# Attention in a hybrid decoder block on Trainium2: four of the six q and k copies between partition halves as DMAs from ScalarE's queue

## The chip, the cores and the metric

The kernel runs on one core of one Trainium2 chip. The metric is the device time of one execution in microseconds (us); less is better. Of the kernel before there are three timed runs and one profiled execution.

## The reference, cut to what matters

One decoder block over 1024 tokens of width 1024, in float32. Three groups of heads share one input projection: a gated short convolution, a stick-breaking attention (8 heads of 64), and a spatial gating unit. Their outputs are joined and projected, then follow a feed-forward block of width 4096 with a squared ReLU, and a gated layer embedding. The change lies in the attention:

```python
q = rms_norm(q.reshape(bsz, s_len, ATTN_HEADS, HEAD_DIM), q_norm_g[i])
k = rms_norm(k.reshape(bsz, s_len, ATTN_HEADS, HEAD_DIM), k_norm_g[i])
...
z = jnp.einsum('bqhd,bkhd->bhqk', qi, kj) * scale
t_pos = start + jnp.arange(Q_BLOCK)[:, None]
s_pos = jnp.arange(end)[None, :]
causal = s_pos < t_pos
log_beta = jax.nn.log_sigmoid(z)
log_rem = jnp.where(causal, jax.nn.log_sigmoid(-z), 0.0)
suffix = lax.cumsum(log_rem, axis=3, reverse=True) - log_rem
weights = jnp.where(causal, jnp.exp(log_beta + suffix), 0.0)
o = jnp.einsum('bhqk,bkhd->bqhd', weights, vj)
```

The kernel takes suffix products of sigmoid(−z) with a scan instead of sums of logarithms.

## The kernel before, in words

**Precision.** TensorE multiplies numbers of a reduced float32 format (fp32r). A float32 value is split into a high part (a ScalarE copy that rounds, L134 or L137) and a low part (a VectorE subtraction, L135 or L138). A product of two split values is three matmuls, high·high, low·high and high·low (`product`, L161 to L163).

**Head pairs.** The 8 heads are worked on in 4 pairs. `project(pr)` loads the weights of a pair (SP's queue, 8 loads of 128x384, L66) and computes for each of 8 blocks of 128 tokens the columns of q, k and v into a PSUM bank `qkv_ps` (24 matmuls). ScalarE squares (L338), VectorE sums, POOL takes the power −1/2 (`rs`, L169), VectorE scales q and k (`qk`, L346). V is split straight from the bank (ScalarE L137, VectorE L138); only then is the bank free. There are two such banks.

**Turning q and k.** After every second block, `turn_qk` transposes q and k of two blocks on TensorE into a PSUM bank `qk_tr`, so that the partitions hold the 2 × 64 head dimensions: head 0 in partitions 0 to 63 (`lo_p`), head 1 in 64 to 127 (`hi_p`). It writes the high parts of q to `QS[0]`, the low parts to `low_q`, the high parts of k to `KH[0]`, and the low parts of k to `KL` (VectorE, L371), whose other half is zero.

**The operands of z.** z = q·k needs three products per head, over 64 dimensions each, but the array has 128 rows. So two products are stacked in one matmul: for each head a tile `QS` holds q's high part in one half of the partitions and q's low part in the other, and `KH` holds k's high part in both. z is then QS·KH (L409) plus QS·KL (L411), and a mask matmul (L415). To stack them, parts must move from one half of the partitions to the other. That is the place of the change, reached once per head pair and half of the tokens (`t % 4 == 3`), 8 times. The eight places lie near 105, 127, 167, 200, 237, 270, 306 and 345 us. Before, six copies of 64x512 are done there, three on ScalarE (L375 to L377) and three on VectorE (L378 to L380). Four of the six change partitions: L376 and L377, L379 and L380. L375 and L378 stay in the same partitions.

**Attention.** `attend(pr)` goes through 8 steps (2 heads × 4 groups of two blocks). `stick` makes z in a PSUM bank (two banks `z`), two sigmoids on ScalarE (L416, L417), a scan on VectorE (L421) and a product on POOL or VectorE (L424). `gather` transposes the weights (`w_tr`, L446), splits them (L134, L135) and multiplies with V (`av`, L464). ScalarE copies the result to `y_both` (L473), POOL adds its two halves by a DMA (L475), SP stores it (L395).

**Other transfers in that time.** `block_sums` prepares sums of the last weights in DRAM: 16 copies of 1 MB from ScalarE's queue (`w_sums<-in_w_ff`, L300) and 16 adding transfers of 1 MB from POOL's queue (L297), tied to the steps of `attend`. SP's queue loads weights into a ring of 7 `stage` tiles (L66).

**The order of work.** The Python code weaves `attend(pr)` with the fill, `project(pr + 1)` and at last the convolution, by counts of matmuls. A scheduler then reorders the instructions of each engine by a model of time. So what an engine does next is fixed in the program, and each engine works through its own row in order. DMAs are issued by an engine's sequencer in that same order. A DMA of SP's or ScalarE's queue reports its end on one of 8 counters, DMAHW0 to DMAHW7, which the program deals out in turn; a DMA that gets a counter waits until the last transfer on that counter has landed, and the engine that issues it waits with it.

Of the kernel before, what the change touches and what calls it, by code (L numbers as in the profile page):

```python
# [7 lines left out]
F32 = mybir.dt.float32  # L8
# [24 lines left out]
def hybrid_block(ctx: ExitStack, tc: tile.TileContext, a: dict):  # L33
# [5 lines left out]
    nc = tc.nc  # L39
# [42 lines left out]
    def bank(pool, s):  # L82
        return pool.tile([P, HT], F32, tag=pool.name, name=name(s))
# [47 lines left out]
    def split(src, hi, lo, scale=None, low=nc.vector):  # L131

        if scale is None:
            nc.scalar.copy(hi, src)  # L134
            low.tensor_tensor(out=lo, in0=src, in1=hi, op=ALU.subtract)  # L135
        else:
            nc.scalar.activation(hi, src, AF.Copy, scale=scale)  # L137
            nc.vector.scalar_tensor_tensor(out=lo, in0=src, scalar=scale, in1=hi,  # L138
                                           op0=ALU.mult, op1=ALU.subtract)
# [91 lines left out]
    lo_p, hi_p = slice(0, HD), slice(HD, P)  # L231
# [75 lines left out]
    def project(pr):  # L307
# [11 lines left out]
        for t in range(KT):  # L319
# [34 lines left out]
            if t % 2 == 1:  # L354
                later(72, lambda t=t, qk=qk: turn_qk(heads[pr], t, qk))

    def turn_qk(head, t, qk):

        QS, KH, KL, _, low_q = head
        th = t // 4  # L360
        tr = bank(ps_tr, "qk_tr")
        for i in range(2):
            for j in range(2):
                o = j * 256 + i * P
                nc.tensor.transpose(tr[:, o:o + P], qk[:, i, j * P:(j + 1) * P], ident)
        ws = slice((t % 4 - 1) * P, (t % 4 + 1) * P)

        split(tr[:, :256], QS[0][th][:, ws], low_q[th][:, ws], scale=gq)
        nc.scalar.activation(KH[0][th][:, ws], tr[:, 256:], AF.Copy, scale=gk)
        for hh, own in enumerate((lo_p, hi_p)):  # L370
            nc.vector.scalar_tensor_tensor(out=KL[hh][th][own, ws], in0=tr[own, 256:],  # L371
                                           scalar=gk[own], in1=KH[0][th][own, ws],
                                           op0=ALU.mult, op1=ALU.subtract)
        if t % 4 == 3:
            nc.scalar.copy(KH[1][th][hi_p], KH[0][th][hi_p])  # L375
            nc.scalar.copy(KH[1][th][lo_p], KH[0][th][hi_p])  # L376
            nc.scalar.copy(KH[0][th][hi_p], KH[0][th][lo_p])  # L377
            nc.vector.tensor_copy(QS[1][th][hi_p], QS[0][th][hi_p])  # L378
            nc.vector.tensor_copy(QS[1][th][lo_p], low_q[th][hi_p])  # L379
            nc.vector.tensor_copy(QS[0][th][hi_p], low_q[th][lo_p])  # L380
        return 8

    PROJECT = KT * 72 + 32
# [310 lines left out]
    def fetch(src, tag="raw"):  # L694
        t = late_slot(tag, "raw")
        nc.sync.dma_start(t, src)
        return t
# [142 lines left out]
    for h in range(2):  # L840
        for n in (0, 4, 1, 5, 2, 6, 3, 7):
# [11 lines left out]
            if h == 0:  # L853
                i = len(y_parts[1])
                src = fetch(y_dram[i, 1], "sum") if i < 6 else y_a[i - 6][1]
# [262 lines left out]
```

## Time and profile before

| | us |
|---|---|
| Timed runs, median | 1238.73 |
| Timed runs, lowest and highest | 1237.89, 1245.04 |
| Profiled execution, its time | 1241.13 |
| Profiled execution, span | 1239.4 |
| TensorE busy in the span | 1208.5 |
| VectorE busy | 869.2 |
| ScalarE busy | 605.0 |
| POOL busy | 357.4 |

The mean granted TensorE clock of the span is 0.985 of full speed. The attention takes roughly the stretch from 105 to 370 us; what follows (output projection, feed-forward block, embedding) is not touched. In the rows of the profile PE is TensorE's matmuls, PEld its weight loads, DVE VectorE, ACT ScalarE, POOL GpSimd, SP SyncE; a name with q (ACTq) is the engine's sequencer. "out<-in" are the program's tile names, "<-DVE QS L380" behind an idle time is what ended it. A row of DMA issues gives the time of the issue, and under it the time from issue to landing, as minimum, median and maximum.

### The profile page before, as it was taken

How to read it: one execution, taken by the hardware profiler on the slowest of the kernel's cores; microseconds unless marked ns; L12 is line 12 of the kernel's file. 1: busy time of each engine (PE TensorE's matmuls, PEld its weight loads, DVE VectorE, ACT ScalarE, POOL GpSimd, SP SyncE). 2: the span in 40 equal slices, each digit the busy share in tenths (PEclk: the TensorE clock that was granted, in tenths of full speed). 3: DMA queues.
4: the chain of work that ended last, by engine and by line, in shares of the span. 5: the costliest groups of instructions: out<-in, count | busy, mean ns of one | idle time of the engine just before them, and what ended most of it. 6: DMA issues, size and time to landing. Idle time of an engine off the chain costs nothing.

```text
span 1239.4 us, 17510 instructions
## 1 busy us (share of the span) xinstructions
PE 1208.5 (98%) x5868; PEld 1032.3 (83%) x5868; DVE 869.2 (70%) x1268; ACT 605.0 (49%) x1199; POOL 357.4 (29%) x361
## 2 busy tenths in 40 slices
PE   8999899999999999889999999999999999999998
PEld 7899899898988788678888888888888888888887
DVE  7846888878789655767877678687665555796443
ACT  7736766667565365643333433355453444455211
POOL 2324335465322223235535435321000000022110
PEclk9999999999999999989999999999999999999999
DMA  8602349998631398799999999868865664643221
GB/s 293 237 18 96 117 159 262 246 184 148 129 75 35 116 298 225 205 231 264 269 260 241 254 251 244 234 232 283 327 212 195 199 218 161 224 157 96 83 103 51
DMA packets 119754, 236.46 MB, mean 191 GB/s; under 512 B 13392, under 2 KB 20816, under 8 KB 119408
## 3 DMA queue, kind: packets, MB, share of 16 engines
q1 hardware_dynamic: 94848, 168.08, 40.7%
q0 software_dynamic: 24304, 50.49, 20.6%
q10 hardware_dynamic: 512, 16.78, 3.7%
q8 instruction: 46, 0.75, 0.2%
q14 instruction: 44, 0.36, 0.1%
HBM read 176.57 MB, written 78.64 MB: 206 GB/s over the span
## 4 chain that ended last, share of the span: by engine, by line
PE 85%; DVE 6%; issue 3%; DMA 3%; POOL 2%; ACT 2%; SPq 0%; POOLq 0%; DVEq 0%; ACTq 0%
PE d_ps L752 25%; PE f_ps L752 24%; PE qkv_ps L161 3%; PE qkv_ps L162 3%; PE qkv_ps L163 3%; PE g_ps L161 2%; PE g_ps L163 2%; PE g_ps L162 2%; DVE rem L421 2%; PE av L464 2%; PE w_tr L446 2%; PE o_ps L161 1%; PE o_ps L162 1%; PE o_ps L163 1%; PE cv_ps L161 1%
## 5 line engine op out<-in xcount | busy, mean ns | idle before, releaser
L135 DVE TENSOR_TENSOR w_lo<-raw,w_hi 128x512 fp32r<-128x512 f32 x268 | 240.7, 900 | 94.4 <-ACT w_hi L134 93.1
L134 ACT CAST w_hi<-raw 128x512 fp32r<-128x512 f32 x268 | 164.9, 619 | 241.2 <-PE d_ps L752 119.2
L752 PE MATMUL f_ps<-hn_hi,w_hi 128*128 128x512 f32 x448 | 176.5, 394 | 5.0 <-ACT v L905 5.0
L752 PE MATMUL f_ps<-hn_lo,w_hi 128*128 128x512 f32 x448 | 175.8, 392 | 0.0
L752 PE MATMUL f_ps<-hn_hi,w_lo 128*128 128x512 f32 x448 | 175.3, 392 | 0.0
L752 PE MATMUL d_ps<-f_hi,w_hi 128*128 128x512 f32 x448 | 174.3, 389 | 0.0
L752 PE MATMUL d_ps<-f_lo,w_hi 128*128 128x512 f32 x448 | 174.3, 389 | 0.0
L752 PE MATMUL d_ps<-f_hi,w_lo 128*128 128x512 f32 x448 | 174.3, 389 | 0.0
L421 DVE TENSOR_TENSOR_SCAN rem<-rem 128x128 f32<-128x128 f32 (+3 forms) x64 | 91.5, 1434 | 19.5 <-ACT rem L416 18.5
L752 PEld LDWEIGHTS f_ps<-hn_hi,w_hi 128*128 128x128 f32 x448 | 85.0, 190 | 23.4 <-ACT v L905 5.5
L752 PEld LDWEIGHTS f_ps<-hn_hi,w_lo 128*128 128x128 f32 x448 | 85.1, 190 | 18.0
L740 POOL TENSOR_TENSOR S<-S,sq 128x512 f32<-128x512 f32 x14 | 20.5, 1463 | 275.7 <-ACT sq L809 275.7
L752 PEld LDWEIGHTS f_ps<-hn_lo,w_hi 128*128 128x128 f32 x448 | 85.1, 190 | 17.8 <-issue 0.2
L752 PEld LDWEIGHTS d_ps<-f_lo,w_hi 128*128 128x128 f32 x448 | 84.1, 188 | 17.6
L752 PEld LDWEIGHTS d_ps<-f_hi,w_hi 128*128 128x128 f32 x448 | 84.1, 188 | 17.4
L752 PEld LDWEIGHTS d_ps<-f_hi,w_lo 128*128 128x128 f32 x448 | 84.1, 188 | 17.3
L161 PE MATMUL qkv_ps<-whi,xn_hi 128*128 128x384 f32 x256 | 92.5, 361 | 1.9 <-DVE V L138 1.8
L162 PE MATMUL qkv_ps<-wlo,xn_hi 128*128 128x384 f32 x256 | 89.8, 351 | 0.0
L163 PE MATMUL qkv_ps<-whi,xn_lo 128*128 128x384 f32 x256 | 89.3, 349 | 0.0
L135 DVE TENSOR_TENSOR f_lo<-raw,f_hi 128x512 fp32r<-128x512 f32 x112 | 78.6, 731 | 4.2 <-ACT f_hi L134 3.9
L134 ACT CAST f_hi<-raw 128x512 fp32r<-128x512 f32 x112 | 67.1, 620 | 17.0 <-DMA raw<-f_dram 13.8
L424 POOL TENSOR_TENSOR wt<-wt,rem 128x127 f32<-128x127 f32 (+4 forms) x40 | 45.9, 1156 | 82.7 <-DVE rem L421 40.6
(220 smaller groups left out, 2650.3 us busy)
## 6 DMA issues: line engine op xcount, KB each, us to landing
raw<-in_w_ff SPq DMA_DIRECT2D x160, 256.0 KB, 4.1
raw<-f_dram SPq DMA_DIRECT2D x112, 256.0 KB, 4.6
raw<-w_sums SPq DMA_DIRECT2D x64, 256.0 KB, 3.7
f_dram<-f SPq DMA_DIRECT2D x48, 256.0 KB, 4.6
f_dram<-t SPq DMA_DIRECT2D x48, 256.0 KB, 4.1
w_sums<-in_w_ff POOLq DMA_DIRECT2D x8, 1024.0 KB, 11.4
w_sums<-w_sums POOLq DMA_DIRECT2D x8, 1024.0 KB, 12.3
raw<-in_w_ff POOLq DMA_DIRECT2D x32, 256.0 KB, 5.1
```

Source lines behind the costliest of these rows:

```text
L134: nc.scalar.copy(hi, src)
L135: low.tensor_tensor(out=lo, in0=src, in1=hi, op=ALU.subtract)
L161: nc.tensor.matmul(ps, lh, rh, start=first and i == 0, stop=False)
L162: nc.tensor.matmul(ps, lh, rl, start=False, stop=False)
L163: nc.tensor.matmul(ps, ll, rh, start=False, stop=last and i == len(terms) - 1)
L421: nc.vector.tensor_tensor_scan(out=back, data0=back, data1=back, initial=1.0, op0=ALU.mult, op1=ALU.bypass)
L424: done = (nc.vector if on_vector else nc.gpsimd).tensor_tensor(out=wt[:, :W - 1], in0=wt[:, :W - 1], in1=rem[:, 1:W], op=ALU.mult)
L446: nc.tensor.transpose(tr[:, n:n + P], wts[i][:, kb * P:(kb + 1) * P], ident)
L464: nc.tensor.matmul(av[:, first * P:], lhs, part[:, o:o + m], start=kb == 0 and part is hi, stop=kb == 2 * g + 1 and part is lo)
L740: return eng.tensor_tensor(out=out, in0=x, in1=y, op=ALU.add)
L752: nc.tensor.matmul(bank, l, r, start=first and k == 0 and i == 0, stop=k == len(b) - 1 and i == 2, skip_group_check=True)
```

## The change

Of the six copies the two that stay in their partitions (L375 and, now on ScalarE, `QS[1][hi_p]`) are ScalarE copies. The four that change partitions become DMAs of 64x512 float32 (128 KB), all issued by ScalarE's queue. One of them, `KH[1][lo_p]`, now reads the tile that the first ScalarE copy has just written. VectorE keeps none of the six. Nothing else in the source is changed.

```diff
         if t % 4 == 3:
             nc.scalar.copy(KH[1][th][hi_p], KH[0][th][hi_p])
-            nc.scalar.copy(KH[1][th][lo_p], KH[0][th][hi_p])
-            nc.scalar.copy(KH[0][th][hi_p], KH[0][th][lo_p])
-            nc.vector.tensor_copy(QS[1][th][hi_p], QS[0][th][hi_p])
-            nc.vector.tensor_copy(QS[1][th][lo_p], low_q[th][hi_p])
-            nc.vector.tensor_copy(QS[0][th][hi_p], low_q[th][lo_p])
+            nc.scalar.copy(QS[1][th][hi_p], QS[0][th][hi_p])
+
+            for to, src in ((KH[1][th][lo_p], KH[1][th][hi_p]), (KH[0][th][hi_p], KH[0][th][lo_p]),
+                            (QS[1][th][lo_p], low_q[th][hi_p]), (QS[0][th][hi_p], low_q[th][lo_p])):
+                nc.scalar.dma_start(to.bitcast(F32), src.bitcast(F32))
```

The scheduler moves other work in answer. The rows below are the engines' orders at two of the eight places; a number behind a tile's name tells its copies apart, and the waits are those that the program sets. The copies of the change are rows L375 to L377 before, and L375, L376 and L380 after.

ScalarE at the fourth place (second head pair, second half of the tokens), before:

```order
L369 ACTIVATE KH_1801<-qk_tr_2279,c_gk 128x256 [waits DVE_49]
L375 COPY KH_1805<-KH_1801 64x512 [waits Activation_49]
L376 COPY KH_1805<-KH_1801 64x512
L377 COPY KH_1801<-KH_1801 64x512 [waits DVE_49,Activation_49]
L137 ACTIVATE V_2372<-qkv_ps_2265,r_566 128x2x64 [waits DVE_49]
L134 CAST wT_hi_2437<-w_tr_2432 128x512 [waits PE_49]
```

and after:

```order
L369 ACTIVATE KH_1801<-qk_tr_2279,c_gk 128x256 [waits DVE_49]
L375 COPY KH_1805<-KH_1801 64x512 [waits Activation_49]
L376 COPY QS_1804<-QS_1802 64x512
L380 DMA QS_1804<-q_lo_1803 64x512 [waits DMAHW1_49]
L380 DMA KH_1805<-KH_1805 64x512 [waits DMAHW2_49,Activation_49]
L380 DMA KH_1801<-KH_1801 64x512 [waits DMAHW3_49,DVE_49]
L380 DMA QS_1802<-q_lo_1803 64x512 [waits DMAHW5_49,Activation_49]
L137 ACTIVATE V_2372<-qkv_ps_2265,r_566 128x2x64
L473 COPY y_both_2386<-av_87 128x256 [waits PE_49]
```

Four DMAs, each with a wait for a counter, now stand between the copies and V. The transfers that used counters 1, 2, 3 and 5 last before them are, in SP's order after, the loads of stage_3109, stage_3115, stage_3121 and stage_4001. TensorE at the same place, before:

```order
L446 MATMUL w_tr_2447<-ident,wt_2328 128x128 [waits PE_49]
L446 MATMUL w_tr_2447<-ident,wt_2338 128x128 x2
L409 MATMUL z_2390<-KH_1801,QS_1802 128x128 [waits DVE_49,Activation_49]
L411 MATMUL z_2390<-KL_1797,QS_1802 128x128
L415 MATMUL z_2390<-below,ident 128x128
L409 MATMUL z_2396<-KH_1406,QS_1802 128x512
L411 MATMUL z_2396<-KL_1402,QS_1802 128x512
L161 MATMUL qkv_ps_2469<-whi_2210,xn_hi_197 128x384 [waits DVE_49]
```

and after (the 24 matmuls of qkv_ps_2469 and some others lie in the piece left out):

```order
L446 MATMUL w_tr_2447<-ident,wt_2328 128x128 [waits PE_49]
L446 MATMUL w_tr_2447<-ident,wt_2338 128x128 x2
L161 MATMUL qkv_ps_2469<-whi_2210,xn_hi_197 128x384 [waits DVE_49]
...
L464 MATMUL av_87<-wT_hi_2451,V_1700 128x128
L464 MATMUL av_87<-wT_lo_2452,V_1700 128x128
L409 MATMUL z_2390<-KH_1801,QS_1802 128x128 [waits DMAHW5_49,DMAHW3_49]
L411 MATMUL z_2390<-KL_1797,QS_1802 128x128
```

The first z of the place has moved back by 32 rows, from row 1024 of TensorE to row 1056, behind the next block's qkv_ps, whose bank is the one that V_2372 empties. TensorE at the sixth place (third pair, second half), before:

```order
L161 MATMUL qkv_ps_3346<-whi_3087,xn_hi_197 128x384 [waits DVE_49]
L162 MATMUL qkv_ps_3346<-wlo_3088,xn_hi_197 128x384
L163 MATMUL qkv_ps_3346<-whi_3087,xn_lo_198 128x384
L409 MATMUL z_3287<-KH_2674,QS_2675 128x128 [waits Activation_49]
L411 MATMUL z_3287<-KL_2670,QS_2675 128x128
```

and after:

```order
L161 MATMUL qkv_ps_3346<-whi_3087,xn_hi_197 128x384 [waits DVE_49]
L162 MATMUL qkv_ps_3346<-wlo_3088,xn_hi_197 128x384
L163 MATMUL qkv_ps_3346<-whi_3087,xn_lo_198 128x384
...
L464 MATMUL av_87<-wT_lo_3358,V_2578 128x128
L409 MATMUL z_3287<-KH_2674,QS_2675 128x128 [waits DMAHW5_49,DMAHW4_49]
L411 MATMUL z_3287<-KL_2670,QS_2675 128x128
```

Here z has moved back by 28 rows, from 1442 to 1470, and waits for two of the four transfers.

## The prediction

> **What bounds the kernel now.** I read the page's busy shares first, then busy time by stretches, because the change works only in the first third of the span: the copies in question run from about 105 to 347 us.
>
> ```profile
> PE 1208.5 (98%) x5868; PEld 1032.3 (83%) x5868; DVE 869.2 (70%) x1268; ACT 605.0 (49%) x1199; POOL 357.4 (29%) x361
> 118.00:345.00 227.00, 215.42 (x1328) 203.00 (x1326) 186.63 (x285) 149.35 (x378) 104.81 (x103) 0.95 0.74 183
> 198.00:218.00 20.00, 19.02 (x125) 18.04 (x123) 15.49 (x23) 14.64 (x38) 8.46 (x9) 1.00 0.80 241
> 220.00:230.00 10.00, 7.99 (x40) 7.51 (x40) 9.56 (x12) 4.18 (x10) 3.55 (x4) 0.83 1.13 207
> ```
>
> A window's row gives its length, then busy PE, PEld, DVE, ACT and POOL with their counts, the granted TensorE clock, the DMA share and GB/s. Over the span TensorE is full. In the attention stretch (second row) it stands 227.00 − 215.42 = 11.6 us in all, and the clock there is 0.95. All that a faster VectorE can give back lies in those 11.6 us and that clock. VectorE is 82% busy there, ScalarE 66%, so VectorE is the tighter of the two helpers, and in single windows (last row: 9.56 of 10) it is the bound. Next come the waits of TensorE between 100 and 350 us (total, times, longest):
>
> ```profile
> PE w_tr L446 <- DVE KL L371: 3.7, 3, 1.7
> PE qkv_ps L161 <- DVE V L138: 1.8, 1, 1.8
> PE z L409 <- DVE QS L380: 1.0, 1, 1.0
> ```
>
> Only the last names a removed copy directly. The others may stand behind one, which the chain of waits tells (start, us, engine, line):
>
> ```profile
> 199.42 0.42 DVE QS L379
> 200.33 0.43 DVE QS L380
> 200.90 0.30 PE z L409
> ...
> 269.76 0.35 DVE QS L378
> 270.13 0.43 DVE QS L379
> 270.59 0.42 DVE QS L380
> ...
> 271.45 0.65 PE qkv_ps L161
> ...
> 306.80 0.91 DVE QS L378
> 307.73 0.42 DVE QS L379
> ```
>
> So VectorE's copies lie on the path at three of the eight places (four head pairs, two halves of the tokens): the fourth, near 200 us, the sixth, near 270, and the seventh, near 307.
>
> **The change, part by part.** *Removed.* Per place three VectorE copies and, net, one of ScalarE's three go:
>
> ```profile
> L376 ACT CAST KH<-KH x8: 617/618/621, 105.3 to 345.7; 64x512 fp32r<-64x512 f32 x8
> L378 DVE CAST QS<-QS x8: 419/420/983, 105.8 to 344.4; 64x512 fp32r<-64x512 f32 x8
> ```
>
> VectorE loses 24 × 0.42 = 10.1 us of work. That is the ceiling of the gain. Most of it is not on the path. What is: at the sixth place 0.35 + 0.43 + 0.42 = 1.2 us, since TensorE's 1.8 us wait for V at 271.45 has the three copies ahead of V on VectorE; at the seventh 0.91 + 0.42 = 1.3 us. The fourth place's 1.0 us is dealt with below. Credit: −2.5 us.
>
> *Added on ScalarE.* Four issues of DMAs of 128 KB per place. The trace of before has no such transfer between partitions from ScalarE's queue. The nearest rows are ScalarE's own issues of 1 MB transfers, and SP's stores of the same 64x512 shape:
>
> ```profile
> L300 ACTq DMA_DIRECT2D w_sums<-in_w_ff x16: 496/548/1101, 117.8 to 241.4; - x16
> DMA to landing us min/median/max: 5.8/7.9/10.7
> ...
> L395 SPq DMA_DIRECT2D y_dram<-y_both x12: 445/451/777, 137.5 to 350.1; - x12
> DMA to landing us min/median/max: 2.2/2.7/8.6
> ```
>
> An issue takes about 0.55 us of ScalarE's order of work, so ScalarE goes from three copies (1.85 us) to two copies and four issues (1.24 + 2.2 = 3.4 us): 1.6 us more a place. ScalarE is busy 14.64 of 20 us around the fourth place; this hides. A landing is bounded by 2.2 from below and 10.7 from above. In a quiet stretch I take 2.7, the same shape's median. Before, z needed 3 × 0.42 us of copies; now it needs a landing, so the program's order has put z later, behind 28 to 32 other matmuls at the fourth and sixth places. These cover a short landing.
>
> The Trainium skill ("DMA: Bandwidth & Descriptors", section "Anatomy of one DMA — SWDGE (gpsimd) path") fits a transfer as 2.0 us plus its bytes over 436 GB/s, which makes 2.3 us of 128 KB, an estimate by that page. The trace agrees where the engines are idle (2.2 us at least) and not in the two jams below; by the page alone both would cost nothing, and the time of the first rival below would hold.
>
> *The fourth place: a wait for a completion counter.* In the changed order ScalarE's four issues wait for counters 1, 2, 3 and 5, and the transfers that hold these are SP's loads of the next weights. When these landed before:
>
> ```profile
> L66 SPq DMA_DIRECT2D stage<-in_w_qkv x2: 328/368/407, 190.2 to 190.6; - x2
> DMA to landing us min/median/max: 7.0/10.7/14.4
> ...
> L66 SPq DMA_DIRECT2D stage<-in_w_qkv x2: 328/368/407, 190.6 to 191.3; - x2
> DMA to landing us min/median/max: 14.4/15.0/15.5
> ...
> L66 SPq DMA_DIRECT2D stage<-in_w_conv x1: 382/382/382, 192.2 to 192.2; - x1
> DMA to landing us min/median/max: 15.5/15.6/15.8
> ...
> L137 ACT ACTIVATE V<-qkv_ps,r x1: 367/367/367, 200.3 to 200.3; 128x128 fp32r<-128x128 f32 x1
> ```
>
> The last of the four holders, the load of in_w_conv, landed at 192.2 + 15.5 = 207.7. ScalarE reaches the issues at about 199.5, so it would stand there for 8 us. Queued right behind is V (last row: 200.3 before), which empties the PSUM bank that the next qkv_ps needs, and the next qkv_ps now stands ahead of z on TensorE. So: 207.7, + 0.5 for the issue, + 0.4 for V on ScalarE, + 0.4 for V's low part on VectorE = 209.0. TensorE's first new work was z at 200.90; it now is qkv_ps at 209.0: **+8.1**, in which before's 1.0 us is already replaced. Then the clock. After the 1.8 us stand at 271.45 it was:
>
> ```profile
> 271.00:274.00 3.00, 2.55 (x8) 2.39 (x9) 2.27 (x6) 2.12 (x7) 1.03 (x1) 0.59 1.13 208
> 274.00:277.00 3.00, 3.00 (x16) 2.97 (x15) 1.73 (x2) 1.34 (x3) 0.45 (x1) 0.84 1.13 207
> ```
>
> That is 3 × 0.41 + 3 × 0.16 = 1.7 us lost: **+1.7**. Some comes back: while TensorE stands, VectorE and POOL catch up, and the next stall that VectorE causes, the 2.0 us of the window 220 to 230 above, can shrink or vanish: between 0 and −2.0; I take **−2.0**, as VectorE has far more slack than that in 8 us. Fourth place: +7.8. The bounds are a load that lands before 199.5 (−1.0, the old stall gone) and none of it given back (+9.8).
>
> *The sixth place: the transfers' own landing.* Here z waits for them in a jam that POOL's adding 1 MB transfers make:
>
> ```profile
> 257.60 2.46 POOL L297 DMA_DIRECT2D w_sums<-w_sums  x2
> ...
> L297 POOL DMA_DIRECT2D w_sums<-w_sums x8: 1069/1263/1817, 224.5 to 380.3; - x8
> DMA to landing us min/median/max: 8.0/12.0/22.1
> ...
> L66 SPq DMA_DIRECT2D stage<-in_w_conv x8: 327/328/382, 250.3 to 258.1; - x8
> DMA to landing us min/median/max: 2.4/2.5/7.4
> ...
> 269.41 0.62 ACT L376 CAST KH<-KH 64x512 fp32r<-64x512 f32 x1
> 272.53 0.31 PE L409 MATMUL z<-KH,QS 128*128 128x128 f32 x1
> ```
>
> POOL's second add of that pair, issued about 258.8, lands about 22.1 later, at 280.9; the windows above show a DMA share of 1.13 through 277. SP's load issued as this begins took 7.4 us, where its fellows took 2.5. ScalarE's second copy ended at 270.0; three issues later, at about 271.5, the fourth goes out. By the 7.4 it lands at 278.9, by the 10.7 at 282.2. z is due at 272.5 − 1.2 (the credit) + 28 × 0.17 (the rows moved ahead of it; the 198 to 218 row has 19.02/125 = 0.15, the 274 to 277 row, at a clock of 0.84, 3.00/16 = 0.19) = 276.1. So TensorE stands between 2.8 and 6.1 us; four transfers at once rather than one load speak for more than 2.8, and I take the middle, **+4.5**. The clock after this stand costs what it costs now after the 1.8 us one: 0.
>
> *The other places.* At the second, ScalarE waits for counters held by SP's loads again:
>
> ```profile
> L66 SPq DMA_DIRECT2D stage<-in_w_qkv x2: 328/538/747, 119.3 to 119.7; - x2
> DMA to landing us min/median/max: 8.8/8.8/8.8
> ```
>
> These land by 128.5, about 1 us after ScalarE comes; between 0 and 1: **+0.5**. At the first, third, fifth and eighth places z comes late enough after the copies to cover a 2.7 us landing: 0.
>
> *Sum.* +7.8 (fourth) + 4.5 (sixth) + 0.5 (second) − 2.5 (credits) = +10.3 us. The profiled execution took 1241.13 us (span 1239.4); it would be 1251.4. That execution is 2.4 us over the median of the runs shown, 1238.73; on the median I predict **1249.0 us**.
>
> **The rivals.** *Both waits are hidden, and the freed VectorE shows.* If SP's loads of the fourth place land before 199.5, as the first of them did (190.2 + 7.0 = 197.2), and ScalarE's queue is served at the sixth as in a quiet stretch (2.7 us: 274.2, ahead of 276.1), only gains are left: −2.5 and the 1.0 us stall for QS, −3.5: 1235.2 us. For it speaks that the order of loads can shift by microseconds when ScalarE's own 1 MB transfers go out at other moments; against it, that three of the four loads landed between 205 and 208, not by chance but behind POOL's and ScalarE's megabytes.
>
> *ScalarE's transfers stay behind POOL's until the jam ends; slower than I forecast.* At the sixth place z then waits until 280.9 + 2.2 = 283.1, a stand of 7.0 instead of 4.5; with TensorE stopped twice for so long, POOL's adds, whose starts hang on ScalarE's and POOL's own work, run later too, and the stall of 220 to 230 stays (+2.0). Sum +14.8: 1253.5 us, slower than before by 1.2%. It decides as soon as the fourth transfer takes over 11 us. For it: the 22.1 us landing, and the loads that took 15 near 192. Against: the 7.4 of SP's load in the same jam.
>
> *The change moves nothing.* ScalarE gets to the issues later than I think, so that its stand is short, and the freed VectorE time meets other waits (ScalarE's sigmoids): 1238.7 us. The trace speaks against it only through the order of the program, which puts V straight behind the waits.
>
> **How the numbers follow.** My forecast 0.43, hidden waits 0.22, the long jam 0.25, nothing moves 0.10. The likeliest case spans 1243 to 1253 by its bounds. The range must reach to the hidden case (1235, less 2 for credits at places I counted as nothing) and past the long jam (1253.5, and some 5 more if the counters at other places wait too): 1233 to 1259. About 1% is what a measurement of this kernel can tell from no change: 1226.3 and 1251.1. Slower by more: most of the long jam (0.22) and the upper quarter of my own case (0.11), 0.33. Faster by more needs over 12 us, more than all of TensorE's standing in the stretch: 0.04. Within: 0.63.
>
> **What would show it.** Right: near 200 us ScalarE stands for about 8 us ahead of the fourth place's issues, V comes about 208 instead of 200.3, TensorE's row of qkv_ps there carries an idle of 8 us put down to V, and the clock of the next 3 us falls to about 0.6. Near 276 the first z carries an idle of 3 to 6 us with a DMA as releaser, and the transfers' landing is over 7 us there and under 3 in quiet stretches. VectorE's busy time falls by about 10 us, ScalarE's by about 5. Wrong: if ScalarE passes the fourth place in under 2 us, the counter wait is not where I put it; if the transfers land in 3 us near 271, the jam doesn't touch ScalarE's queue; if TensorE's standing between 118 and 345 us falls below 11.6 us, the credits were larger than the chain shows.

## The result and the profile after

The changed kernel takes 1256.84 us (median of 4 runs, 1255.42 to 1258.81), the kernel before 1238.31 (median of 4, 1233.79 to 1245.04). The ratio is 1.0146, with a 95% interval from 1.0098 to 1.0195: slower by 18.5 us. The forecast was 1249.0, slower by 10.3 us, with a range from 1233 to 1259. The two profiled executions, 1255.42 and 1241.13 us, differ by 14.3 us; the traces can explain that much.

The page's first row after, and the window from 190 to 220 us before (second row) and after (third row), with busy PE, PEld, DVE, ACT, POOL and their counts, the clock, the DMA share and GB/s:

```profile
PE 1206.0 (96%) x5868; PEld 1027.0 (82%) x5868; DVE 861.3 (69%) x1244; ACT 600.0 (48%) x1191; POOL 360.7 (29%) x361
190.00:220.00 30.00, 28.64 (x180) 26.67 (x178) 24.92 (x39) 21.11 (x55) 16.76 (x17) 1.00 0.94 259
190.00:220.00 30.00, 20.67 (x120) 20.16 (x121) 13.87 (x26) 11.62 (x33) 9.45 (x11) 0.83 0.72 194
```

VectorE did lose 8 us of work and ScalarE 5, as the change says. But in the window after TensorE is busy 20.67 of 30 us, where it was busy 28.64 before. The waits of TensorE between 100 and 400 us after (total, times, longest):

```profile
PE qkv_ps L161 <- DVE V L138: 11.3, 4, 8.8
PE av L464 <- DVE wT_lo L135: 3.0, 3, 2.0
...
PE av L464 <- ACT y_both L473: 1.5, 1, 1.5
PE z L409 <- DMA QS<-q_lo: 1.5, 1, 1.5
```

The first row is the new one: a wait for V that was 1.8 us in all before is 11.3, and one of its four is 8.8 us long. This is where it lies, in the timeline after:

```profile
199.09 0.49 ACTq L380 DMA_DIRECT2D QS<-q_lo  x1
...
199.72 0.50 ACTq L380 DMA_DIRECT2D KH<-KH  x1
...
202.94 0.47 ACTq L380 DMA_DIRECT2D KH<-KH  x1
...
208.65 0.47 ACTq L380 DMA_DIRECT2D QS<-q_lo  x1
209.16 0.37 ACT L137 ACTIVATE V<-qkv_ps,r 128x128 fp32r<-128x128 f32 x1 [8.95 <-DMA KH<-KH]
...
209.56 0.35 DVE L138 SCALAR_TENSOR_TENSOR V<-qkv_ps,r,V 128x128 fp32r<-128x128 f32 x1 [9.35 <-ACT V L137]
...
209.97 0.69 PE L161 MATMUL qkv_ps<-whi,xn_hi 128*128 128x384 f32 x1 [8.79 <-DVE V L138]
```

ScalarE issues two of the fourth place's transfers at once, the third at 202.94 and the fourth at 208.65. Only then come V, its low part, and TensorE's next qkv_ps. And these are the SP loads whose counters the third and the fourth issue wait for, with their times to landing:

```profile
L66 SPq DMA_DIRECT2D stage<-in_w_qkv x1: 328/328/328, 191.3 to 191.3; - x1
DMA to landing us min/median/max: 11.6/11.6/11.6
...
L66 SPq DMA_DIRECT2D stage<-in_w_conv x1: 392/392/392, 192.2 to 192.2; - x1
DMA to landing us min/median/max: 16.4/16.4/16.4
```

191.3 + 11.6 = 202.9 and 192.2 + 16.4 = 208.6: each issue follows its load's landing within 0.1 us.

To see how much each stretch loses, I laid the two kernels over each other by TensorE's work: for a time of the kernel before, the time at which another kernel has done the same number of matmul columns since 90 us, counted from the rows of TensorE. The differences, in us (the two kernels do the work in another order, which makes a single value uncertain by about 1, and by several us where the orders are far apart, as at 150 or 220):

| before at | 110 | 130 | 160 | 190 | 200 | 230 | 280 | 330 | 390 |
|---|---|---|---|---|---|---|---|---|---|
| the change | +1.5 | +3.2 | +3.0 | +3.8 | +14.5 | +16.2 | +15.1 | +15.9 | +15.6 |

So about +1.5 come at the first place, where TensorE stands 0.6 us for a V that is queued behind ScalarE's issues, some +2 at the second, +10.7 between 190 and 200 at the fourth, +1.7 more until 230, and little is won or lost from there on. The second place, after:

```profile
126.33 0.49 ACTq L380 DMA_DIRECT2D QS<-q_lo  x1
127.28 1.14 ACTq L380 DMA_DIRECT2D KH<-KH  x2
128.51 0.56 ACTq L380 DMA_DIRECT2D QS<-q_lo  x1
129.11 0.37 ACT L473 COPY y_both<-av 128x256 f32<-128x256 f32 x1 [3.03 <-DMA QS<-q_lo]
...
129.54 0.39 PE L464 MATMUL av<-wT_hi,V 128*128 128x256 f32 x1 [1.54 <-ACT y_both L473]
```

A like thing on a smaller scale: y_both stands 3.0 us on ScalarE behind the issues, and TensorE 1.5 us behind y_both. But here the waits for counters are the small part: the four issues themselves take 2.2 of the 3.0 us (0.49, 1.14 for two, 0.56).

### The profile page after: what moved, and what is told of

Same layout as the page of the kernel before. It is cut to its first block, busy times and chain, and to the rows that moved or that the text cites. A ratio compares the mean times of both kernels' runs of the same rounds, so it can differ in the third digit from the quotient of the medians.

```text
span 1253.7 us, 17563 instructions
## 1 busy us (share of the span) xinstructions
PE 1206.0 (96%) x5868; PEld 1027.0 (82%) x5868; DVE 861.3 (69%) x1244; ACT 600.0 (48%) x1191; POOL 360.7 (29%) x361
## 4 chain that ended last, share of the span: by engine, by line
PE 83%; DMA 6%; DVE 4%; issue 3%; ACT 2%; POOL 2%; ACTq 0%; SPq 0%; POOLq 0%; DVEq 0%
PE d_ps L752 24%; PE f_ps L752 24%; PE qkv_ps L161 2%; PE g_ps L161 2%; PE g_ps L163 2%; PE g_ps L162 2%; PE qkv_ps L162 2%; PE qkv_ps L163 2%; PE av L464 2%; PE w_tr L446 2%; PE cv_ps L161 2%; PE cv_ps L162 2%; PE cv_ps L163 2%; PE o_ps L161 1%; PE o_ps L163 1%
## 5 line engine op out<-in xcount | busy, mean ns | idle before, releaser
L161 PE MATMUL qkv_ps<-whi,xn_hi 128*128 128x384 f32 x256 | 90.2, 352 | 11.4 <-DVE V L138 11.3
L169 POOL TENSOR_TENSOR rs<-ss,mhalf 128x4 f32<-128x4 f32 x32 | 44.2, 1381 | 94.4 <-DVE ss L341 94.3
## 6 DMA issues: line engine op xcount, KB each, us to landing
w_sums<-in_w_ff POOLq DMA_DIRECT2D x8, 1024.0 KB, 11.3
```

The source lines that it names most:

```text
L161: nc.tensor.matmul(ps, lh, rh, start=first and i == 0, stop=False)
L169: nc.gpsimd.tensor_tensor(out=out, in0=in_, in1=mhalf[:, :n], op=ALU.pow)
```

## The experiments

The theory to test (theory 1): the loss is ScalarE's standing in order, at the issue of a transfer, for a counter that an SP load holds, with work that TensorE needs queued behind it. The rivals: the transfers' own landings (theory 2), or the rearranged order and ScalarE's added work, wherever the copies stand (theory 3). Medians of before in the two sets were 1238.67 (21 runs) and 1238.91 us (23 runs).

**The fourth place undone.**

```diff
-        if t % 4 == 3:
+        if t % 4 == 3 and (pr, th) == (1, 1):
+            (the six copies of before)
+        if t % 4 == 3 and (pr, th) != (1, 1):
             (two copies, four transfers)
```

> The change at seven places; only at the fourth (second head pair, second half of the tokens) the six copies of before stand. Theory 1 (the loss is ScalarE's stand at the fourth place behind counters that SP's loads hold, with V queued behind it: 8.8 us of TensorE's standing and about 1.7 us of lower clock): about 10 us come back, 1246 to 1248 us; V of that place starts near 200 and the 8.8 us idle is gone. Theory 2 (each place costs about the same, by the issues on ScalarE and by landings that z waits for): one eighth of 18 us comes back, 1254 to 1255. Theory 3 (the rearranged order costs, wherever the transfers stand): 1254 to 1260.

Measured: 1243.73 us (7 runs), ratio to before 1.0039 [1.0023, 1.0055]. Of the 18 us, 13 came back. The window from 190 to 220 us:

```profile
190.00:220.00 30.00, 28.79 (x187) 27.28 (x185) 24.11 (x36) 18.84 (x51) 14.62 (x17) 1.00 0.93 264
```

TensorE is at 28.79 of 30 again, and the clock at 1.00 in place of 0.83. It is more than theory 1 asked for, and far from what theories 2 and 3 did.

**The fourth place alone.** The same edit with the two conditions exchanged.

> The change at the fourth place alone; the six copies of before at the other seven. Theory 1: nearly the whole loss of the stand, 9 to 11 us over before: 1247 to 1250 us, with one idle of 8 us of TensorE on V near 200. Theory 2: an eighth of the loss, 1240 to 1242. Theory 3: near before, 1237 to 1242.

Measured: 1248.24 us (5 runs), ratio 1.0083 [1.0054, 1.0113], 9.6 us over before. ScalarE's wait and the window:

```profile
ACT V L137 <- DMA KH<-KH: 9.1, 1, 9.1
```

```profile
190.00:220.00 30.00, 20.84 (x119) 20.33 (x118) 12.37 (x22) 9.93 (x27) 8.89 (x12) 0.83 0.68 188
```

One place of eight, with four transfers, carries over half of the loss. Undone it gives 13.1, alone it costs 9.6: the two need not agree, since the orders differ elsewhere too.

**The transfers from SP's queue.**

```diff
-                nc.scalar.dma_start(to.bitcast(F32), src.bitcast(F32))
+                nc.sync.dma_start(to.bitcast(F32), src.bitcast(F32))
```

> All four transfers of every place go out from SP's queue in place of ScalarE's. Theory 1: SP stands for the same counters until about 207 at the fourth place, but V is not behind it, so the idle of qkv_ps on V is gone; z, 44 matmuls after that qkv_ps (due near 208), may wait for a landing between 209.6 and 215: 2 to 7 us in place of 8.8. In all 1248 to 1254 us. Theory 2 (landings): as the change, 1256 to 1258, with the waits on z. Theory 3 (order): 1255 to 1260.

Measured: 1244.12 us (9 runs), ratio 1.0053 [1.0034, 1.0071]: less than expected, and 12.7 us less than the change with the same bytes moved. TensorE's waits from 190 to 232 us, and SP's longest from 186 to 212:

```profile
PE z L409 <- DMA QS<-q_lo: 4.4, 1, 4.4
...
PE qkv_ps L161 <- DVE V L138: 0.4, 1, 0.4
```

```profile
SPq L395 <- DMA y_both<-y_both: 16.4, 1, 16.4
```

V no longer waits. SP does stand, and until 207, as expected, but that hit is luck, for it is not for the counters: they were dealt out anew, and the loads that hold the four have landed by 197.4. SP stands 16.4 us ahead of a store of y_both, which waits for POOL's adding transfer, and the four issues follow that store from 207.73 on. They land 2.3 us after issue, so the 4.4 us that z waits are the late issue and not a long landing: theory 2, as a cost of landings, is not seen here. By work this kernel is level with before until 200 (−0.6), which says that the loss at the first two places, too, came from issuing on ScalarE's queue; then +8.2 at 230, and +3.9 at 330.

**No transfer at all.**

```diff
-            nc.vector.tensor_copy(QS[1][th][hi_p], QS[0][th][hi_p])
-            nc.vector.tensor_copy(QS[1][th][lo_p], low_q[th][hi_p])
-            nc.vector.tensor_copy(QS[0][th][hi_p], low_q[th][lo_p])
+            nc.scalar.copy(QS[1][th][hi_p], QS[0][th][hi_p])
+            nc.scalar.copy(QS[1][th][lo_p], low_q[th][hi_p])
+            nc.scalar.copy(QS[0][th][hi_p], low_q[th][lo_p])
```

> No transfer at all: all six copies on ScalarE. VectorE is freed exactly as by the change (24 copies), and ScalarE gets 3 copies more a place (1.85 us, where the change gave it about 1.6). Theory 1: no counter, no stand: the credit of 2.5 us less what ScalarE's longer work costs, 1235 to 1241 us. Theory 2: the landings are gone, the same 1235 to 1241. Theory 3 (ScalarE's added work and the rearranged order cost the time): 1248 to 1258.

Measured: 1245.05 us (9 runs), ratio 1.0047 [1.0027, 1.0066]. Here theory 1 as I put it missed: it gave up to 1241. With VectorE freed by 24 copies and no transfer to wait for, the kernel is 6.4 us slower than before, not faster. Two of its idles of TensorE:

```profile
224.76 0.63 PE L446 MATMUL w_tr<-ident,wt 128*128 128x128 f32 x4 [2.15 <-DVE KL L371]
...
274.12 0.69 PE L161 MATMUL qkv_ps<-whi,xn_hi 128*128 128x384 f32 x1 [2.46 <-DVE V L138]
```

The sixth place's wait for V, from which I took a credit of 1.2 us, has grown from 1.78 to 2.46: what VectorE no longer has ahead of V's low part, ScalarE now has ahead of V. So a few more microseconds on ScalarE are not free, though it is busy only two thirds of the time. Theory 3 expected 1248 to 1258 and missed on the other side.

**The megabytes put off.** The changed kernel, with the 1 MB transfers put off by four steps from the attention's step 6 on (the last four steps' follow the attention).

```diff
+    pending = list(range(8 * 4))
...
-            block_sums(8 * pr + i, (last_pool[0], last_act[0]))
+            if not 6 <= 8 * pr + i <= 9:
+                block_sums(pending.pop(0), (last_pool[0], last_act[0]))
...
+        while pr == 3 and pending:
+            block_sums(pending.pop(0), (last_pool[0], last_act[0]))
```

> The changed kernel, with the 1 MB transfers of two steps (POOL's two adds issued near 184 us and ScalarE's two copies near 195) put off by four steps, and so all later ones; the last follow at the end of the attention. ScalarE's four issues of the fourth place still wait for counters that SP's loads hold. Theory 1 with the jam (those loads land late because of the megabytes around them): they land in 2.5 to 6 us, ScalarE stands at most 2 us, the 8.8 us idle of TensorE is gone, and the kernel takes 8 to 12 us less than the change: 1244 to 1249 us, if the moved transfers hurt nowhere else; the next kernel shows that. Rival (the loads are late by their own queue, or the wait is for something other than their landing): the stand stays, 1255 to 1259 us.

Measured: 1251.73 us (4 runs), ratio 1.011 [1.0087, 1.0133]. The loads near the fourth place, and ScalarE there (the edit shifts line numbers by one):

```profile
L66 SPq DMA_DIRECT2D stage<-in_w_qkv x3: 327/386/539, 187.1 to 189.3; - x3
...
L66 SPq DMA_DIRECT2D stage<-in_w_conv x1: 402/402/402, 190.0 to 190.0; - x1
...
DMA to landing us min/median/max: 2.4/2.5/2.6
```

```profile
194.83 0.49 ACTq L381 DMA_DIRECT2D QS<-q_lo  x1
...
195.82 0.49 ACTq L381 DMA_DIRECT2D KH<-KH  x1
196.41 0.55 ACTq L381 DMA_DIRECT2D KH<-KH  x1
197.06 0.67 ACTq L381 DMA_DIRECT2D QS<-q_lo  x1
198.28 0.37 ACT L137 ACTIVATE V<-qkv_ps,r 128x128 fp32r<-128x128 f32 x1
```

The loads land in 2.5 us in place of 11.6 to 16.4, ScalarE's four issues follow one another, and by work the kernel is at +3.6 at 200 and +2.0 at 230, where the change is at +14.5 and +16.2. The stand is gone. It is not the jam alone that differs: the counters were dealt out anew (the loads that hold them had landed by 189.6), and other work stands between the issues and V. The total lies above the band of 1244 to 1249. By work the kernel loses some 9 us between 280 and 290, where the control, below, loses 8, and some 6 more after 390, where the control loses under 1. The latter was not looked into.

**The control: the same megabytes put off in the kernel before.** The same edit on before.

> The kernel before, with the same steps' 1 MB transfers put off in the same way. A control: it waits for no load at the fourth place. Theory 1: within 4 us of before, 1235 to 1243. Rival (the megabytes cost by themselves): as much less than before as the kernel above is less than the change.

Measured: 1244.11 us (8 runs), ratio 1.0052 [1.0035, 1.0069]; 1 us outside theory 1's band, and on the other side of the rival, which wanted it faster. Moving the megabytes costs 5 us by itself. Near 284 ScalarE's V waits for a store of y_both, and TensorE stands 5.1 us behind it:

```profile
ACT V L137 <- DMA y_dram<-y_both: 6.0, 1, 6.0
```

Between the two kernels with the megabytes moved lie 7.6 us, between the change and before 18.5. The difference, about 11 us, is what hangs on the late loads by this pair, and a rough figure, as the 7.6 hold the loss after 390.

**The second and the fourth place undone.** As the first, with both places excluded.

> The change at six places; the six copies of before at the second and the fourth. Where it stands beside the kernel that undoes the fourth alone (1243.7): by the work done on TensorE that one had fallen 4 us behind before between 110 and 160 us, where ScalarE stood for counters at the second place, y_both waited 3 us behind it and TensorE 1.5 us. Theory 1 (ScalarE's stands are the loss): 2 to 4 us less, 1239.5 to 1242. Theory 3 (the rest is the rearranged order): 1242 to 1248.

Measured: 1237.37 us (10 runs), ratio 0.9989 [0.9975, 1.0003]. A further 6.4 us came back, 2 more than theory 1's band, and theory 3, as a loss wherever the transfers stand, is out: six of eight places run as changed, in a rearranged order, and no loss is left. By work it stands at −0.7 at 160 (the first experiment was at +4.3). What the second place adds is ScalarE's queue, but, by the rows above, more the issues than the waits for counters; so the expectation's reason, the stand for counters, is right only in part.

**SP's queue at seven places, the fourth undone.** The edits of the first and the third together.

> The transfers from SP's queue at seven places, and the copies of before at the fourth. With them at all eight from SP's queue the kernel took 1244.1, of which TensorE stood 4.4 us for a transfer's landing at the fourth place and lost about 8 us between 200 and 230; it made up 4 us between 240 and 330. Theory 1: no place stands; if the 4 us come from the freed VectorE, 1234 to 1238, faster than before. If they were only the catching up after the stand, 1238 to 1241. Theory 3 (order): 1242 to 1246.

Measured: 1234.63 us (10 runs), ratio 0.9966 [0.9951, 0.9981]: 4.3 us faster than before, the only kernel of the study clear of it on that side. TensorE's waits from 95 to 390 us (the edit shifts line numbers behind L380 by seven: L453 is L446 of before, L431 is L424, L471 is L464, L416 is L409, L424 is L417):

```profile
PE w_tr L453 <- DVE wt L431: 2.9, 4, 1.2
PE av L471 <- DVE wT_lo L135: 2.7, 2, 2.0
PE w_tr L453 <- DVE KL L371: 1.7, 1, 1.7
PE w_tr L453 <- ACT wt L424: 1.5, 1, 1.5
PE z L416 <- ACT wt L424: 1.3, 4, 0.4
PE z L416 <- ACT KH L377: 1.0, 1, 1.0
```

No wait for V and none for a landing is left. By work: +1.4 at 230, −4.3 at 330, a gain of 5.7 us in the stretch of the fifth to seventh places. The same work there, in before and in this kernel:

```profile
230.00:330.00 100.00, 95.96 (x608) 91.82 (x607) 82.70 (x133) 68.60 (x173) 47.32 (x46) 0.95 0.78 173
231.40:325.70 94.30, 91.49 (x605) 87.18 (x604) 79.53 (x126) 64.67 (x166) 47.04 (x48) 1.00 0.86 196
```

TensorE stands 2.8 us in place of 4.0, and the clock is 1.00 in place of 0.95, which is some 5 us of the 100: most of the gain is the clock. In before it was 0.83 from 270 to 280 and 0.71 from 310 to 320, each time after TensorE had stood. Before's waits of TensorE for V and KL in this stretch (1.8 and 0.9 us, both on VectorE) are gone, which fits the freed VectorE; that ScalarE has one copy less a place, and the other order, were not told apart from it.

## Why the prediction was right or wrong

**Right: the mechanism and its place.** V started at 209.16 where I had 208.2, the next qkv_ps at 209.97 where I had 209.0, with an idle of 8.79. Undoing that place, doing it alone, and lifting the jam each show it. The clock during the stand, and in the first three microseconds after it, where I had expected about 0.6:

```profile
203.00:209.00 6.00, 0.00 (x0) 0.00 (x0) 0.00 (x0) 0.00 (x0) 0.00 (x0) 0.54 0.68 180
210.00:213.00 3.00, 3.00 (x9) 3.00 (x10) 1.91 (x4) 1.22 (x5) 1.01 (x1) 0.50 0.11 25
```

The stand and the clock, +8.1 and +1.7, made 9.8; by work it was 10.7.

**Wrong: the give-back of 2.0 us.** I let VectorE's catching up during the stand shrink the next stall. It didn't: from 200 to 230 another 1.7 us were lost. The sum missed by 3.7 us there. VectorE did not catch up: from 203 to 209 (first row above) it and POOL were busy 0.00 of 6 us, like ScalarE and TensorE. Having slack was not the question; nothing was ready for it. Waits for wT_lo (2.0 us) and wT_hi (1.6) then took the place of the one before. That their inputs hang on ScalarE's copies and on TensorE's own matmuls, which stood too, is read from the order, not tested.

**Wrong in size: the second place, and the first.** I took +0.5 at the second, half of a stand of 1 us. y_both stood 3.0 us on ScalarE; by work the place cost some 2 us in the changed kernel, 5 in the kernel with the fourth undone (+4.3 at 160 against −0.7), and undoing it there gave 6.4 us. I priced only the wait for the counters, not the issues with it (2.2 us in the rows above), and not that y_both, on which TensorE's next av waits, is queued there. The first place, which I put at 0 because z comes late enough, lost 1 to 1.5 us because V, not z, is queued behind the issues.

**Wrong in size, on the other side: the sixth place.** I expected z to stand 4.5 us. After:

```profile
L380 ACTq DMA_DIRECT2D QS<-q_lo x2: 495/524/552, 281.6 to 283.9; - x2
...
DMA to landing us min/median/max: 5.5/6.0/6.8
```

```profile
290.81 0.30 PE L409 MATMUL z<-KH,QS 128*128 128x128 f32 x1 [1.52 <-DMA QS<-q_lo]
```

The four transfers landed in 5.5 to 6.8 us; the row that I had given less weight, SP's load in the same jam with 7.4, was nearer than ScalarE's megabyte with 10.7. The stand was 1.5. The rival of the long jam, which needed over 11 us, did not happen.

**Wrong: the credit of 2.5 us.** From 230 to 330 the changed kernel gained 0.3 us net of the 1.5 at the sixth place, about 1.8 gross. The same stretch of work as above, in the changed kernel:

```profile
246.20:345.90 99.70, 93.05 (x603) 87.44 (x602) 81.06 (x126) 64.74 (x168) 47.27 (x49) 1.00 0.85 189
```

I had counted the copies' own time on the path and no clock with it. The clock is the larger part: here too it is 1.00 in place of 0.95. But TensorE now stands 6.7 us in place of 4.0, which takes about half of that back; where the other half goes was not traced. At the seventh place V waits on ScalarE behind the issues, and TensorE behind V:

```profile
323.45 0.37 ACT L137 ACTIVATE V<-qkv_ps,r 128x128 fp32r<-128x128 f32 x1 [1.80 <-issue]
...
324.26 0.45 PE L161 MATMUL qkv_ps<-whi,xn_hi 128*128 128x384 f32 x1 [1.24 <-DVE V L138]
```

I had let the 1.6 us more of ScalarE a place hide because it was busy 14.64 of 20 us. Where V stands behind it, it does not hide. With the issues on SP's queue this stretch gains 5.7 us, against the 2.5 that I had in all.

**The range and the rivals.** 1256.84 lies in the range, near its upper end and above the likeliest case's own 1243 to 1253. Slower by over 1% had 0.33. That the forecast came as near as it did is partly luck: the sixth place, put 3 us too high, made up for most of what the give-back hid. The rival of hidden waits fell with the stand; its price, 3.5 us faster than before, is close to what the last experiment measured (4.3) once the waits were taken out, though by another sum, most of it the clock. The long jam's 1253.5 is nearer than my 1249.0, but of its two terms only one came true: the stall of 220 to 230 was not given back; the long landing at the sixth place did not come. That the change moves nothing fell too.

**What stays open.** The fourth place undone gives 13 us, alone it costs 9.6: how much of the difference is order, and how much is that a late kernel meets other transfers, was not separated. Nor was it shown why the kernel with six ScalarE copies loses 6.4 us beyond the two stalls quoted. Why the kernel with the megabytes put off loses some 6 us after 390 is open too. And the medians lie 18.5 us apart, the profiled executions 14.3. Of these 4.2 us, 2.6 lie in the first 20 us of the span, far ahead of the change. Before (first row) and after there:

```profile
0.00:20.00 20.00, 16.54 (x64) 13.78 (x65) 10.79 (x19) 13.15 (x24) 6.75 (x20) 0.91 0.76 233
0.00:20.00 20.00, 17.74 (x76) 14.99 (x77) 12.29 (x21) 14.15 (x26) 7.21 (x21) 1.00 0.85 276
```

The profiled execution of before had a lower clock and a less busy TensorE here, and was 2.6 us behind by work at 20 us. The table above counts from 90 us, so this plays no part in it.

## What to carry to other kernels

A transfer is not free for the engine that issues it: besides its 0.5 us it can wait there, in order, for whatever the program hung on its completion counter, here another queue's load of 16 us, and everything behind it waits too. Even without that wait, four issues of 0.5 us ahead of something that TensorE needs cost time. Before moving a copy to a DMA, read in the program's order what each new issue waits for, when that landed in the old trace, and what stands right ahead of and behind the issue: on SP's queue it was a store ahead that made it late. Then choose the queue whose followers nobody needs soon, keep the plain copy where the issue or the landing would be late, and price a stall that goes or comes with the clock that follows it: the same idea was 1.5% slower on ScalarE's queue at eight places and 0.3% faster on SP's at seven.

## What the runs showed of the hardware that I had not expected

SP's last four loads of 192 KB ahead of the fourth place took 7.8 to 16.4 us to land near POOL's and ScalarE's megabytes, and 2.4 to 2.6 with these put off, a factor of three to six. Transfers of 128 KB between partitions took 2.2 us in quiet stretches and at most 8.1 in the changed kernel, also at the fourth place, where SP's loads had taken up to 16.4 us a little earlier. TensorE's granted clock was 0.59 from 271 to 274 in before, after a stand of only 1.8 us; from 230 to 330, at a clock of 0.95, the lowered clock cost some 5 us and the stands themselves 4.0.
